# A fixed order of TensorE's phases in a mixture-of-experts kernel, with an expert's return in two halves inside the next expert

## The chip, the cores and the metric

The kernel runs on one core of a Trainium2 chip. The metric is the device time of one execution in microseconds, taken as the median of the runs shown. TensorE does the matmuls, VectorE (DVE), ScalarE (ACT) and GpSimd (POOL) the element-wise work, and SyncE (SP) issues the transfers of the weights.

## The reference, cut to what matters

A layer of a streaming encoder over 256 tokens of width 2048, all in float32: a mixer (attention beside a state-space scan), then 16 experts with two chosen per token, beside a gated per-layer embedding (PLE), and a normalisation behind each half. The change touches what comes after the mixer:

```python
def routed_experts(x, w_router, router_bias, w_gate, w_up, w_down):
    ...
    for e in range(N_EXPERTS):
        hid = jax.nn.silu(xt @ w_gate[e]) * (xt @ w_up[e])
        out = out + combine[:, e:e + 1] * (hid @ w_down[e])

def per_layer_embedding(x, p_i, w_ple, w_ple_gate):
    gate = jax.nn.sigmoid(jnp.einsum('bsd,de->bse', x, w_ple_gate))
    return gate * jnp.einsum('bsk,kd->bsd', p_i, w_ple)

        h = layer_norm(DEEPNORM_ALPHA * h + mix, ln1_g[i], ln1_b[i])
        moe = routed_experts(h, ...)
        ple = per_layer_embedding(h, p[i], w_ple[i], w_ple_gate[i])
        h = layer_norm(DEEPNORM_ALPHA * h + moe + ple, ln2_g[i], ln2_b[i])
```

## The kernel before

**Stages.** The mixer runs to about 429 us, the first normalisation and the router to about 458, the sixteen experts to about 1454, and the second normalisation and the output end the span at 1475.1.

**One expert.** An expert works on up to 64 of the 256 tokens. `gather` (L678 to L703) picks the rows of two experts at once by 32 matmuls of `h` with a one-hot tile `oh` (L692), so it runs ahead of experts 0, 2, 4 and so on; ScalarE and VectorE copy the result into `xg`. `gate_up` (L714 to L725) multiplies `xg` with eight weight tiles of 2 MiB, alternately of w_gate and w_up (L722, 64 matmuls, 128 instructions in the trace). `places` (L705 to L712) transposes the one-hots (L709) into `cm`. `hidden` (L727 to L737) forms silu(gate) x up (L729 to L731), transposes it by four matmuls (L734), and copies it to `hidT` (L736). `down` (L765 to L787) multiplies it with four tiles of w_down (L774, 32 matmuls), splits the product in a high and a low part `y` (L762, L763), and calls `give_back` (L739 to L753): sixteen matmuls of `cm` with `y` (L746) bring the rows back to their tokens, and eight VectorE instructions (L751) drain them, weighted, into `acc`.

**Beside the experts.** `ple_gate` computes a quarter c of the PLE at experts 3, 6, 9 and 12 (`PLE_AT`): 32 sums of hT with three tiles of w_ple_gate (L818, four, eight and four blocks) and eight products with p (L833). The first part of quarter 0 stands behind the router's matmuls (L623), by an `issue_after`. `residual` adds the scaled first normalisation: eight broadcasts of the gain and bias rows per quarter (L898), two VectorE passes (L909, L910), one POOL pass, at experts 4, 5, 7 and 8. At expert 13 the rows of the second norm are made in the same way. At expert 7 `overflow` holds a branch (L848) for experts with over 64 tokens, which isn't taken here.

**The weights.** All weight tiles of this half go through a ring of eight 2 MiB buffers, and one more that is used once. SP issues the loads in the fixed order of `plan_loads`: for each expert g0, u0, ... g3, u3, d0 to d3, and at a PLE expert its three PLE tiles ahead of g0. A load takes the buffer that `take`, in the order of the program, gave back the longest ago, and waits until TensorE has done the last matmul that reads it:

```python
    def fill(self, n=100):
        while self.spare and n and self.n < len(self.loads):
            j = self.spare.pop(0)
            key, load = self.loads[self.n]
            ...
    def take(self, key):
        t, j = self.tiles.pop(key)
        if j != self.once:
            self.spare.append(j)
        return t
```

**What sets the order.** The program text calls the steps expert by expert. Before, the tile scheduler arranges the instructions of each engine by its own estimates; so the PLE sums, the returns of an expert and the next expert's gate stand mixed on TensorE.

## Time and profile before

| | |
|---|---|
| median of 3 runs | 1473.13 us (1471.68 to 1480.07) |
| profiled execution, its own time | 1476.78 us |
| its span | 1475.1 us |
| TensorE busy, 6531 instructions | 1399.1 us, 95% |
| VectorE busy | 465.7 us, 32% |
| ScalarE busy | 297.9 us, 20% |
| weights' queue (q1) | 495.41 MB, 83.8% of 16 engines' span |
| granted clock of TensorE, mean | 0.98 |

The page gives busy time per engine over the whole span. The mixer and the experts have different limits, so the rows further down are of the stretch behind 440 us. [...] Times in rows are microseconds from the span's start.

### The profile page before, as it was taken

The page shows a single profiled execution, that of the slowest core. Times are in us where ns is not written, and L with a number is a line of the kernel's source. Part 1 is how long each engine was busy: PE and PEld are TensorE (multiplying, and loading weights), DVE is VectorE, ACT ScalarE, POOL GpSimd, SP SyncE. Part 2 cuts the span into 40 slices and gives each one's busy share as a digit, 9 for nine tenths or more (in the row PEclk, how much of TensorE's full clock was granted, in tenths as well). Part 3 has the DMA queues.
Part 4 walks back from the last instruction along what each step waited for, and adds up shares of the span by engine and source line. Part 5 has one row for each costly group of instructions (what it writes and reads, how often), then busy time and mean ns, then how long its engine had stood idle before and what let it go on. Part 6 is the DMA issues. An engine that isn't in the chain of part 4 may idle for free. (4 is left out here: it accounts for less than half of the span.)

```text
span 1475.1 us, 15513 instructions
## 1 busy us (share of the span) xinstructions
PE 1399.1 (95%) x6531; PEld 733.8 (50%) x6531; DVE 465.7 (32%) x777; ACT 297.9 (20%) x477; POOL 72.8 (5%) x90
## 2 busy tenths in 40 slices
PE   7999999999989999999999999899999999999994
PEld 5878888787784343334335333433333343353332
DVE  4386774546552211202123002222020220202117
ACT  4475554444340010001001000100010010011001
POOL 3000111201000000000000000000000000000002
PEclk9999999999999999999999999999999999999997
DMA  8645445456939999999999889999999999999993
GB/s 273 195 166 178 160 160 180 157 196 224 344 147 398 426 426 427 416 425 403 425 426 415 322 370 427 375 422 419 399 379 426 427 413 392 420 427 426 426 389 130
DMA packets 89711, 499.93 MB, mean 339 GB/s; under 512 B 9716, under 2 KB 22460, under 8 KB 65316
## 3 DMA queue, kind: packets, MB, share of 16 engines
q1 hardware_dynamic: 88128, 495.41, 83.8%
q0 software_dynamic: 1472, 3.43, 0.8%
q8 instruction: 53, 0.87, 0.2%
q14 instruction: 22, 0.18, 0.0%
q10 hardware_dynamic: 36, 0.05, 0.0%
HBM read 496.70 MB, written 2.16 MB: 338 GB/s over the span
## 5 line engine op out<-in xcount | busy, mean ns | idle before, releaser
L722 PE MATMUL pgu<-ring,xg 128*64 128x512 f32 x2048 | 473.2, 601 | 0.0
L722 PEld LDWEIGHTS pgu<-ring,xg 128*64 128x64 f32 x2048 | 144.4, 138 | 293.3 <-issue 292.5
L774 PE MATMUL py<-ring,hidT 128*64 128x512 f32 x960 | 209.3, 594 | 4.1 <-ACT hidT L736 4.1
L211 DVE TENSOR_TENSOR wl<-ring,wh 128x1024 fp32r<-128x1024 f32 x128 | 156.0, 1223 | 140.2 <-ACT wh L210 135.0
L210 ACT ACTIVATE wh<-ring 128x1024 fp32r<-128x1024 f32 x128 | 135.3, 1059 | 172.5 <-PE pj L217 145.8
L215 PE MATMUL pj<-wh,xh 128*128 128x512 f32 x384 | 154.1, 403 | 0.8 <-ACT xh L192 0.7
L216 PE MATMUL pj<-wl,xh 128*128 128x512 f32 x384 | 153.7, 401 | 0.0
L217 PE MATMUL pj<-wh,xl 128*128 128x512 f32 x384 | 153.1, 400 | 0.0
L730 DVE TENSOR_TENSOR hid<-hid,pgu 128x512 f32<-128x512 f32 x16 | 11.0, 687 | 434.1 <-ACT hid L729 434.1
L774 PEld LDWEIGHTS py<-ring,hidT 128*64 128x64 f32 x960 | 67.6, 137 | 134.8 <-issue 128.5
L818 PE MATMUL pl<-ring,hT 128*128 128x512 f32 x256 | 120.9, 608 | 0.0
L763 DVE TENSOR_TENSOR y<-py,y 128x512 fp32r<-128x512 f32 (+1 forms) x34 | 22.3, 657 | 238.8 <-ACT y L762 238.8
L729 ACT ACTIVATE hid<-pgu 128x512 f32<-128x512 f32 x16 | 9.6, 597 | 401.5 <-PE pgu L722 401.5
L215 PEld LDWEIGHTS pj<-wh,xh 128*128 128x128 f32 x384 | 72.7, 189 | 17.9 <-ACT xh L192 1.8
L217 PEld LDWEIGHTS pj<-wh,xl 128*128 128x128 f32 x384 | 72.6, 189 | 16.7 <-DVE xl L193 0.2
L216 PEld LDWEIGHTS pj<-wl,xh 128*128 128x128 f32 x384 | 72.8, 190 | 16.1
L818 PEld LDWEIGHTS pl<-ring,hT 128*128 128x128 f32 x256 | 45.1, 189 | 64.3 <-issue 64.1
L692 PE MATMUL mt<-oh,h 128*128 128x128 f32 x512 | 63.1, 287 | 5.0 <-PEq L848 5.0
L762 ACT ACTIVATE y<-py 128x512 fp32r<-128x512 f32 (+1 forms) x34 | 19.4, 572 | 229.7 <-PE py L774 200.1
L692 PEld LDWEIGHTS mt<-oh,h 128*128 128x128 f32 x512 | 62.3, 202 | 5.9 <-issue 5.7
L216 PE MATMUL pj<-wl,moh 128*128 128x512 f32 (+1 forms) x160 | 56.6, 354 | 0.5 <-DVE wl L211 0.5
L215 PE MATMUL pj<-wh,moh 128*128 128x512 f32 (+1 forms) x160 | 56.4, 355 | 0.6 <-ACT wh L210 0.6
(260 smaller groups left out, 1005.4 us busy)
## 6 DMA issues: line engine op xcount, KB each, us to landing
ring<-in_w_gate SPq DMA_DIRECT2D x64, 2048.0 KB, 18.2
ring<-in_w_up SPq DMA_DIRECT2D x64, 2048.0 KB, 17.8
ring<-in_w_down SPq DMA_DIRECT2D x60, 2048.0 KB, 16.5
ring<-in_w_in SPq DMA_DIRECT2D x48, 1024.0 KB, 5.1
ring<-in_w_out SPq DMA_DIRECT2D x16, 1024.0 KB, 5.8
ring<-in_w_ple_gate SPq DMA_DIRECT2D x16, 1024.0 KB, 20.6
ring<-in_w_down SPq DMA_DIRECT2D x32, 256.0 KB, 6.0
xq<-in_x SPq DMA_DIRECT2D x8, 256.0 KB, 9.6
```

The costliest lines, as they stand in the source:

```text
L210: nc.scalar.activation(h, v, AF.Copy)
L211: nc.vector.tensor_tensor(l, v, h.bitcast(F32), op=OP.subtract)
L215: nc.tensor.matmul(ps, ah, bh, start=first, stop=False)
L216: nc.tensor.matmul(ps, ah, bl, start=False, stop=False)
L217: nc.tensor.matmul(ps, al, bh, start=False, stop=last)
L692: nc.tensor.matmul(ps[:, k % 4], h[:, t, cols], oh[:, t, :, 0, :], start=t == 0, stop=t == 1)
L722: mm = nc.tensor.matmul(pgu[j][hs], xg[:, k, e % 2, :], w[:, r, fh * 512:(fh + 1) * 512], start=k == 0, stop=k == KB - 1)
L730: nc.vector.tensor_tensor(hid, hid, pgu[0], op=OP.mult)
L762: nc.scalar.activation(yh, ps, AF.Copy)
L763: nc.vector.tensor_tensor(yl, ps, yh.bitcast(F32), op=OP.subtract)
L774: nc.tensor.matmul(py[hs, c, :], hidT[:, j, fh * 64:(fh + 1) * 64], w[:, r, dh * 1024 + c * 512:dh * 1024 + (c + 1) * 512], start=fb == 0, ...
L818: nc.tensor.matmul(pg[t], hT[:, k, t * 128:(t + 1) * 128], w[:, k - k0, :], start=k == 0, stop=k == KB - 1)
```

## The change

**A fixed order.** A context manager `phase()` makes the instructions issued within it stand behind the last TensorE instruction of the phase before. Around `gate_up`, the return's two halves, the hidden transposes, the residual, the gather, the down and the PLE there is one each.

**Returns.** `down` ends with the split of y. An expert's return is made in the next expert's `hidden`: its half c = 0 between gate and hidden transposes, its half c = 1 behind them. The banks of the halves are ("mt", "pl") and ("gu", "mt").

**One-hots.** They are made one expert ahead (`onehot`) in the router's weight tile, no longer for two experts at once, and four small matmuls (L744) transpose them behind the first half of the return.

**PLE.** The quarter is computed in one piece behind the down. The first part of quarter 0 no longer stands behind the router, and its load comes ahead of expert 3, with the two others.

**Residual.** Four transposes of the normalised `hT` per token half take the place of the rows' broadcasts; one VectorE pass adds them to `acc`. It is at experts 2, 4, 5 and 7.

**Rows.** The four rows of gains and biases are no longer loaded in the mixer; those of the second norm are loaded by POOL's queue at expert 13. `hid`, `sg` and others have one buffer in place of two, `cm` has two, and `acc` is opened at expert 1.

```diff
-RES_AT = (4, 5, 7, 8)
+RES_AT = (2, 4, 5, 7)
+LN2_AT = 13
...
-    L.append((("pg", 0, 0), gate_part(0, 0)))
     for e in range(NE):
         if e in PLE_AT:
             c = PLE_AT.index(e)
-            L += [(("pg", c, g), gate_part(g, c)) for g in range(0 if c else 1, 3)]
+            L += [(("pg", c, g), gate_part(g, c)) for g in range(3)]
...
+    place = [None]
+
+    @contextmanager
+    def phase():
+
+        after = tc.issue_after(place[0]) if place[0] else ExitStack()
+        with after:
+            yield
+        place[0] = [i for i in nc.cur_bb.bb.instructions if i.engine == mybir.EngineType.PE][-1]
...
-    def hidden(pgu):
-        hid = mp.tile([128, 512], F32, name="hid", tag="w2", bufs=2)
+    def hidden(e, pgu, oh, between):
+
+
+        hid = mp.tile([128, 512], F32, name="hid", tag="w2", bufs=1)
...
-        ps = mt_psum([128, 4, 128])
+        with phase():
+            between(0)
+        hid_parts = phase()
+        hid_parts.__enter__()
+        ps2 = psum.tile([128, 2, 512], F32, name="py", tag="y", bufs=1)
+        ps, pc = ps2[:, 0, :].rearrange("p (j t) -> p j t", t=128), ps2[:, 1, :256]
+        for t in range(NT):
+            for _, hs in H2:
+                nc.tensor.matmul(pc[hs, t * 128:(t + 1) * 128], oh[:, t, e % 2, :], ident, start=True, stop=True)
...
-        return hidT
+        cm = mp.tile([128, 256], F32R, name="cm", tag="cm", bufs=2)
+        nc.scalar.activation(cm, pc, AF.Copy)
+        hid_parts.__exit__(None, None, None)
+        with phase():
+            between(1)
+        return hidT, cm
...
-        for c in range(2):
-            def pss(t):
-                if t == 0:
-                    return [mt_psum([128, 512]) for _ in range(2)]
-                p2 = psum.tile([128, 2, 512], F32, name="py", tag="y", bufs=1)
-                return p2[:, 0, :], p2[:, 1, :]
-            give_back(e, cm, y, c * 512, 512, pss)
+        return y
+
+    def return_half(e, cm, y, c):
+        def pss(t):
+            tag = (("mt", "pl"), ("gu", "mt"))[c][t]
+            return [psum.tile([128, 512], F32, name="bk", tag=tag, bufs=2) for _ in range(2)]
+        give_back(e, cm, y, c * 512, 512, pss)
...
-    with tc.issue_after(router_mm.ins):
-        ple_sums(0, range(1))
-    xg, oh = gather(0)
...
     def residual(c):
 
-        gain, bias = (row_bank(pl_psum(), lna[:, j, :], c).rearrange("p (f r) -> p r f", r=R) for j in range(2))
-        for t in range(NT):
-            part = mp.tile([128, 512], F32, name="part", tag="w2", bufs=2)
...
+        for t in range(NT):
+            ps = pl_psum()
+            for r in range(R):
+                nc.tensor.transpose(ps[:, r * 128:(r + 1) * 128], hT[:, R * c + r, t * 128:(t + 1) * 128], ident)
+            a = acc[:, t, c * 512:(c + 1) * 512].rearrange("p (f r) -> p r f", r=R)
+            nc.vector.scalar_tensor_tensor(a, ps.rearrange("p (r f) -> p r f", r=R), ALPHA, a, op0=OP.mult, op1=OP.add)
+
+    last = None
     for e in range(NE):
-        pgu, gated = gate_up(e, xg)
-        cm = places(e, oh)
-        hidT = hidden(pgu)
-        if e == 0:
+        if e % 2 and e + 1 < NE:
+            oh_next = onehot(e + 1)
+        with phase():
+            pgu = gate_up(e, xg)
+        if e == 1:
...
+        hidT, cm = hidden(e, pgu, oh, lambda c: last and return_half(*last, c))
         if e in RES_AT:
-            with tc.issue_after(gated.ins):
+            with phase():
                 residual(RES_AT.index(e))
         if e == OV_AT:
             overflow()
+            place[0] = None
+        if e == LN2_AT:
+            lnr = pT[:16].rearrange("p t (j f) -> p t j f", f=128)[:, 0]
+            for j, n in enumerate(("ln2_g", "ln2_b")):
+                nc.gpsimd.dma_start(lnr[:, j, :], i[n][0].rearrange("(k f) -> k f", f=128))
         if e + 1 < NE:
             if e % 2:
-                xg, oh = gather(e + 1)
-            down(e, hidT, cm)
+                with phase():
+                    oh = oh_next
+                    xg = gather(oh)
+            with phase():
+                last = e, cm, down(e, hidT)
...
         if e in PLE_AT:
-            ple_gate(PLE_AT.index(e))
+            with phase():
+                ple_gate(PLE_AT.index(e))
```

On TensorE, at expert 12, before, behind the returns of expert 11 (L818 the PLE sums, L722 the gate's and up's matmuls with the ring's tiles, L734 the hidden transposes, L774 the down):

```order
L709 MATMUL mt<-ident,oh 128x128 x2
L818 MATMUL pl<-ring_6632,hT 128x512 x4
L818 MATMUL pl<-ring_6634,hT 128x512 x8
L722 MATMUL pgu<-ring_6656,xg 64x512 x8
L818 MATMUL pl<-ring_6634,hT 128x512 x3
L722 MATMUL pgu<-ring_6737,xg 64x512 x8
L818 MATMUL pl<-ring_6634,hT 128x512 x3
L722 MATMUL pgu<-ring_6747,xg 64x512 x8
L818 MATMUL pl<-ring_6634,hT 128x512 x2
L818 MATMUL pl<-ring_6653,hT 128x512
L722 MATMUL pgu<-ring_6757,xg 64x512 x8
```

The same place now, from the last of expert 12's gate tiles to the first of expert 13 (L724 the gate's matmuls, L763 a half of the return, L744 the one-hots, L746 the hidden transposes, L790 the down, L832 and L842 the PLE):

```order
L724 MATMUL pgu<-ring_6787,xg 64x512 x8
L763 MATMUL bk<-y_6744,cm 128x512 x8
L744 MATMUL py<-ident,wr 64x128 x4
L746 MATMUL py<-ident,hid 128x128 x4
L763 MATMUL bk<-y_6744,cm 128x512 x8
L790 MATMUL py<-ring_6789,hidT 64x512 x8
...
L832 MATMUL pl<-ring_6579,hT 128x512 x8
L832 MATMUL pl<-ring_6581,hT 128x512 x16
L832 MATMUL pl<-ring_6600,hT 128x512 x8
L842 MATMUL mt<-ring_6600,pT 128x512 x4
L724 MATMUL pgu<-ring_6829,xg 64x512 x8
```

The PLE tiles are the three whose numbers stand ahead of the gate's in the order of the loads; they were read between the gate's tiles, and are read behind the four of the down.

On TensorE, behind the down of expert 13, before (L746 the returns, L722 the gate of expert 14):

```order
L774 MATMUL py<-ring_7076,hidT 64x512 x8
L746 MATMUL mt<-y_7229,cm 128x512 x4
L746 MATMUL mt<-y_7230,cm 128x512
L722 MATMUL pgu<-ring_7094,xg 64x512
L746 MATMUL py<-y_7229,cm 128x512 x4
L746 MATMUL mt<-y_7230,cm 128x512
L746 MATMUL mt<-y_7231,cm 128x512 x2
L722 MATMUL pgu<-ring_7094,xg 64x512 x4
L746 MATMUL py<-y_7230,cm 128x512 x2
L746 MATMUL py<-y_7231,cm 128x512 x2
L722 MATMUL pgu<-ring_7094,xg 64x512 x3
L709 MATMUL mt<-ident,oh 128x128 x2
```

And now, behind the gate of expert 14:

```order
L724 MATMUL pgu<-ring_7205,xg 64x512 x8
L763 MATMUL bk<-y_7207,cm 128x512 x8
L744 MATMUL py<-ident,wr 64x128 x4
L746 MATMUL py<-ident,hid 128x128 x4
L763 MATMUL bk<-y_7207,cm 128x512 x8
L790 MATMUL py<-ring_7278,hidT 64x512 x8
```

The return has left the place behind its own expert's down, and stands around the next expert's hidden transposes.

## Rows read from the trace of the kernel before

**Rows 1.** TensorE's waits from 440 us on: line, releaser, total us, times, longest.

```profile
PE mt L734 <- DVE hid L731: 9.1, 12, 0.8
PE mt L746 <- DVE acc L751: 8.5, 9, 1.0
PE mt L692 <- PEq L848: 5.0, 1, 5.0
```

**Rows 2.** Windows: length, busy us of five engines, granted clock, DMA share, GB/s.

```profile
442.00:1447.00 1005.00, 968.04 (x4386) 385.32 (x4388) 186.36 (x320) 77.33 (x162) 20.73 (x17) 0.98 0.98 408
995.34:1007.39 12.05, 12.05 (x50) 3.79 (x46) 2.42 (x4) 1.19 (x2) 0.00 (x0) 1.00 1.06 402
1125.61:1176.18 50.57, 47.24 (x214) 15.89 (x214) 9.08 (x17) 2.77 (x5) 0.00 (x0) 1.00 1.01 428
```

**Rows 3.** The page: GB/s in 40 equal slices of the span.

```profile
GB/s 273 195 166 178 160 160 180 157 196 224 344 147 398 426 426 427 416 425 403 425 426 415 322 370 427 375 422 419 399 379 426 427 413 392 420 427 426 426 389 130
```

**Rows 4.** Timeline of PE (start, us): hidden transposes, experts 3 and 12.

```profile
663.54 0.74 PE L734 MATMUL mt<-ident,hid 128*128 128x128 f32 x4 [0.79 <-DVE hid L731]
...
1260.26 0.74 PE L734 MATMUL mt<-ident,hid 128*128 128x128 f32 x4 [0.79 <-DVE hid L731]
```

**Rows 5.** Timeline of PE, experts 12 to 15: start, us, instructions.

```profile
1203.30 0.66 PE L746 MATMUL mt<-y,cm 64*128 64x512 f32 x4
...
1205.91 10.47 PE L818 MATMUL pl<-ring,hT 128*128 128x512 f32 x24
1216.30 3.65 PE L722 MATMUL pgu<-ring,xg 128*64 128x512 f32 x16
...
1323.36 7.39 PE L692 MATMUL mt<-oh,h 128*128 128x128 f32 x64
...
1382.77 13.95 PE L774 MATMUL py<-ring,hidT 128*64 128x512 f32 x64 [0.69 <-ACT hidT L736]
...
1434.87 0.44 PE L798 MATMUL py<-ring,hidT 128*64 128x256 f32 x2 [0.69 <-ACT hidT L736]
```

**Rows 6.** Timeline of SP: two loads issued during the gate of expert 14.

```profile
1370.29 0.33 SPq L82 DMA_DIRECT2D ring<-in_w_gate  x1
1373.72 0.33 SPq L82 DMA_DIRECT2D ring<-in_w_up  x1
```

**Rows 7.** DMA issues, 826 to 832 us: size, us from issue to landing.

```profile
ring<-in_w_up SPq DMA_DIRECT2D x1, 2048.0 KB, 7.8
```

**Rows 8.** Groups by line: busy us, mean ns of one, idle before.

```profile
L751 DVE SCALAR_TENSOR_TENSOR acc<-mt,cw,acc 128x512 f32<-128x512 f32 x56 | 40.1, 744 | 6.2 <-PE mt L746 5.9
L898 PE MATMUL pl<-lnr,ident 16*128 16x128 f32 x128 | 17.3, 280 | 0.0
```

**Rows 9.** Timeline of PE at the router.

```profile
442.55 5.40 PE L818 MATMUL pl<-ring,hT 128*128 128x512 f32 x12
448.05 0.37 PE L663 MATMUL mt<-s,tri 128*128 128x16 f32 x2
...
448.71 1.96 PE L818 MATMUL pl<-ring,hT 128*128 128x512 f32 x4
...
457.82 2.37 PE L722 MATMUL pgu<-ring,xg 128*64 128x512 f32 x10
```

**Rows 10.** More windows: TensorE's granted clock is third from last.

```profile
1399.80:1403.20 3.40, 3.40 (x9) 1.37 (x9) 0.90 (x3) 0.00 (x0) 0.00 (x0) 0.51 1.00 422
1396.40:1399.80 3.40, 1.54 (x7) 0.55 (x5) 1.81 (x3) 1.19 (x2) 0.00 (x0) 1.00 1.02 434
1125.60:1129.00 3.40, 1.96 (x10) 1.04 (x12) 0.69 (x1) 0.60 (x1) 0.00 (x0) 1.00 1.04 436
10.00:20.00 10.00, 8.53 (x27) 6.58 (x28) 6.26 (x8) 5.51 (x8) 6.78 (x15) 1.00 1.08 344
```

**Rows 11.** Timeline of SP at the overflow branch of expert 7.

```profile
923.12 0.33 SPq L82 DMA_DIRECT2D ring<-in_w_up  x1
951.97 0.34 SPq L82 DMA_DIRECT2D ring<-in_w_gate  x1
```

More of the change, by code (lines that the diff above doesn't have):

```diff
@@ L1 @@
-from contextlib import ExitStack
+from contextlib import ExitStack, contextmanager
 import concourse.bass as bass
@@ L161, in front @@
     nc.gpsimd.dma_start(cw[80:88], i["ssd_norm_w"][0].rearrange("(b f) -> b f", f=128))
-    lnr = const.tile([16, 4, 128], F32, name="lnr")
-    for j, n in enumerate(("ln1_g", "ln1_b", "ln2_g", "ln2_b")):
-        nc.gpsimd.dma_start(lnr[:, j, :], i[n][0].rearrange("(k f) -> k f", f=128))
-    fr.lnr = lnr
     lnT = const.tile([128, 2, KB], F32, name="lnT")
@@ L622, in back @@
     for t in range(NT):
-        router_mm = nc.tensor.matmul(pr[:, t, :], r4[:, t * 128:(t + 1) * 128], sel4, start=True, stop=True)
+        nc.tensor.matmul(pr[:, t, :], r4[:, t * 128:(t + 1) * 128], sel4, start=True, stop=True)
     rb = fr.rb
@@ L673, in back, with onehot, gather @@
     dbg("pos", pos)
+    place = [None]
[5 more added lines that the diff above has]
+        place[0] = [i for i in nc.cur_bb.bb.instructions if i.engine == mybir.EngineType.PE][-1]
     H2 = ((0, slice(0, 64)), (1, slice(64, 128)))
-    def gather(e):
-        oh = mp.tile([128, NT, 2, 2, CAP], F32, name="oh", tag="oh")
+    def onehot(e):
+        b = e // 2 % 2
+        oh = fr.wr.rearrange("p (b t j k) e -> p b t j (k e)", b=2, t=2, j=2)[:, b]
         for t in range(NT):
             for j in range(2):
-                nc.vector.tensor_scalar(oh[:, t, j], i1[:, None, :].to_broadcast([128, 2, CAP]),
-                                        pos[:, t, e + j:e + j + 1], None, op0=OP.is_equal)
+                nc.vector.tensor_scalar(oh[:, t, j], i1, pos[:, t, e + j:e + j + 1], None, op0=OP.is_equal)
+        return oh
+    def gather(oh):
         xg = mp.tile([128, KB, 2, CAP], F32, name="xg", tag="xg")
@@ L691, in gather @@
                 for t in range(NT):
-                    nc.tensor.matmul(ps[:, k % 4], h[:, t, cols], oh[:, t, :, 0, :], start=t == 0, stop=t == 1)
+                    nc.tensor.matmul(ps[:, k % 4], h[:, t, cols], oh[:, t], start=t == 0, stop=t == 1)
             if k4 % 2:
@@ L702, in gather @@
                 nc.vector.tensor_tensor(v, v, bias, op=OP.add)
-        return xg, oh
-    def places(e, oh):
-        ps = mt_psum([128, 256])
-        for t in range(NT):
-            nc.tensor.transpose(ps[:, t * 128:(t + 1) * 128], oh[:, t, e % 2].rearrange("p a b -> p (a b)"), ident)
-        cm = mp.tile([128, 256], F32R, name="cm", tag="cm")
-        nc.scalar.activation(cm, ps, AF.Copy)
-        return cm
+        return xg
     def gate_up(e, xg):
@@ L755, in y_parts @@
     def y_parts():
-        y0 = mp.tile([128, 2, 512], F32R, name="y0", tag="y")
-        y1 = [mp.tile([128, 512], F32R, name="y1", tag="w2", bufs=2) for _ in range(2)]
-        return (y0[:, 0, :], y0[:, 1, :]), y1
+        y = mp.tile([128, 2, 2, 512], F32R, name="y0", tag="y")
+        return [(y[:, c, 0, :], y[:, c, 1, :]) for c in range(2)]
     def split_y(y, ps, col, n):
@@ L763, in split_y, with down @@
         nc.vector.tensor_tensor(yl, ps, yh.bitcast(F32), op=OP.subtract)
-    def down(e, hidT, cm):
+    def down(e, hidT):
         py = psum.tile([128, 2, 512], F32, name="py", tag="y", bufs=1)
@@ L807, in down_last, with ple_gate @@
                     nc.vector.bn_stats(st[:, t, c, :], acc[:, t, c * 256:(c + 1) * 256])
-    pgs = {}
-    def ple_sums(c, parts):
-        pg = pgs[c] = pgs.get(c) or [pl_psum() for _ in range(NT)]
-        for g in parts:
-            k0, k1 = PLE_PARTS[g]
+    def ple_gate(c):
+        cs = slice(c * 512, (c + 1) * 512)
+        pg = [pl_psum() for _ in range(NT)]
+        for g, (k0, k1) in enumerate(PLE_PARTS):
             w = v2(ring.take(("pg", c, g)), 512)
@@ L821, in ple_sums @@
                 ring.fill()
-        return w[:, k1 - k0:k1 - k0 + 2, :] if k1 == KB else None
-    def ple_gate(c):
-        cs = slice(c * 512, (c + 1) * 512)
-        w = ple_sums(c, range(0 if c else 1, 3))
-        pg = pgs.pop(c)
+        w = w[:, k1 - k0:k1 - k0 + 2, :]
         for t in range(NT):
-            sg = mp.tile([128, 512], F32, name="sg", tag="w2", bufs=2)
+            sg = mp.tile([128, 512], F32, name="sg", tag="w2", bufs=1)
             nc.scalar.activation(sg, pg[t], AF.Sigmoid)
-            ps = pl_psum()
+            ps = mt_psum([128, 512])
             for k in range(2):
@@ L884, in overflow @@
                                                        acc[:, t, cs], op0=OP.mult, op1=OP.add)
-    with tc.issue_after(router_mm.ins):
-        ple_sums(0, range(1))
-    xg, oh = gather(0)
-    lna = fr.lnr[:, 0:2, :]
-    with tc.issue_after(stats_done.ins):
-        nc.vector.tensor_scalar(lna, lna, ALPHA, None, op0=OP.mult)
+    oh = onehot(0)
+    xg = gather(oh)
     def row_bank(ps, rows, c):
```

25 lines of the change are left out of this document (11 added, 14 removed).

## The prediction

> **What bounds the kernel now.** I read the waits first, then the transfers, then the order of time around the four per-layer-embedding (PLE) experts. The waits of TensorE from 440 us on are short and all on its own neighbours: 9.1 us for the hidden product, 8.5 us for the drains of a return, 5.0 us for the overflow branch, others less than 7 [rows 1]. None is on a transfer, so it looks as if TensorE alone set the pace. The windows say that this is only just so. From 442 to 1447 us TensorE is busy 968 of 1005 us, and the transfers run at 408 GB/s in the mean, where the undisturbed expert 11 shows 428 [rows 2] and most slices of the page 425 to 427 [rows 3]. By 427 GB/s the stream has 1005 x (1 - 408/427) = 45 us of idle time in all. A 2 MiB tile (2.097 MB) takes 4.91 us, an expert's twelve take 58.9 us, but TensorE goes through expert 11 in 50.57 us [rows 2]. So in every ordinary expert the stream falls 8 us behind, and it catches up where TensorE works on something else: the PLE sums and the gathers. The eight buffers carry the difference. From the hidden transposes of expert 3 to those of expert 12 the kernel takes 596.7 us, 198.9 for each period of three experts with one PLE part [rows 4]. The stream needs for such a period (the part is 4.72 MB, some 12.05 us by a window in which 402 GB/s moved as much [rows 2]) 3 x 58.9 + 12.05 = 188.8 us. A faster TensorE can therefore gain at most 10 us per period, and only if the stream never stops.
>
> **The change, part by part.** *PLE.* Before, the PLE matmuls stand among the gate's: 1205.91 shows 24 of them, 1216.30 sixteen of the gate, and so on to the hidden transposes at 1260.26 [rows 4, 5]. Each PLE tile is used up, and its buffer given back, while the gate runs. Now the three PLE tiles are still loaded ahead of the gate's first tile, but are taken only after that expert's down. For the gate and the down they occupy three of eight buffers. Two costs follow. First, ahead of the gate's last tile the stream has to bring 12.05 us of PLE data of which TensorE uses nothing yet. Second, after the gate, TensorE works for a long time on tiles that are there (down and PLE), while only the four buffers of the down, and then the PLE's own, come free: the stream stops.
>
> The prices. A PLE matmul takes (1216.30 - 1205.91)/24 = 0.433 us, 72 of them (64 sums, 8 of p) 31.2 us [rows 5]. A gate tile takes 3.43 us, the distance of two issues that each wait for one tile's last matmul [rows 6]; a gate 8 x 3.43 = 27.45. The down takes 13.75, its row less the overlap with the next, the gather 7.2 [rows 5]. A load issued into an idle stream lands 7.8 us later [rows 7].
>
> *Returns.* Before, the sixteen return matmuls begin right after the down, wait for y and for the drains, and the gate's matmuls fill in between; behind the down of expert 14, which ends near 1396.6 [rows 5], TensorE is busy 1.54 of 3.40 us [rows 10]. The change puts eight of them into the wait for the hidden product, and eight into the wait for its copy. Between gate and down there is then 1.33 + 0.45 + 0.74 + 1.33 = 3.9 us: eight returns at twice the row of four (0.66), the one-hots (four with half the columns, 0.37 to 0.74, taken as 0.45) and the four transposes (0.74) [rows 4], eight returns. An ordinary expert takes 27.45 + 3.9 + 13.75 = 45.1 us instead of 50.6. Where a gather follows, its banks come free only behind eight drains of 0.744 us on VectorE [rows 8], 6.0 us against 3.9: I put the lull at 6.5, and with the gather's 7.2 at 13.7. The bounds of that: 3.9 (the drains keep up) to 8 (they start only behind the hidden product).
>
> *Residual, row vectors, one-hots.* Eight transposes, twice 0.74 = 1.5 us, take the place of eight broadcast matmuls (17.3/64 = 0.27 each, 2.2 us [rows 8]), and one VectorE pass that of two and a POOL pass; TensorE's side is what counts, and it gains 0.7 four times, worth nothing where the stream is late anyway. The rows of the second norm come at expert 13 by POOL's queue, 32 such matmuls behind its lull, of which I leave eight to waits that are there anyway: 24 x 0.27 = 6.5 us. The one-hots move one expert earlier on VectorE, at nothing, since it is busy 186 of 1005 us [rows 2].
>
> *Router.* Sixteen PLE matmuls filled the wait for the router: 442.55 and 448.71 [rows 9]. [...] The first gate starts at about 459.3 instead of 457.82 [rows 9].
>
> *The sum*, on the profiled execution's span of 1475.1 us. The first buffer comes free at 459.3 + 3.43 = 462.7; the stream moves from 2.9 us later (7.8 - 4.91). To the gate of expert 3 there are 35 more tiles and the PLE part: 465.6 + 35 x 4.91 + 12.05 = 649.5, and with the last tile's 3.43 the gate ends at 652.9. TensorE alone would be there 20 us earlier, at 459.3 + 43.8 + 54.9 + 46.6 + 27.45 = 632 (expert 0 without returns in its lull, 1 with a gather, 2 with a residual, gate 3). Then 13.7 + 13.75 + 31.2 = 58.7 brings it to 711.6. The last PLE buffer is free only then; its load lands 7.8 later, and 24 tiles and a PLE part follow: 711.6 + 7.8 + 117.8 + 12.05 + 3.43 = 852.7 for the end of gate 6. A period is 199.8 us, against 198.9. Expert 6: 3.9 + 13.75 + 31.2, and 2 for a down tile that isn't there yet, 903.5; gate 7 to 931.0. There the overflow branch stops the stream: SP issues nothing from 923.12 to 951.97 [rows 11], and TensorE loses 5.0 us [rows 1]. With lull, residual and gather (6.5 + 1.5 + 5.0 + 7.2) the down starts at 951.2, its first buffer is free at 954.6, and 16 tiles and a PLE part give 954.6 + 7.8 + 73.7 + 12.05 + 3.43 = 1051.6 for gate 9. One more period: 1251.4 for gate 12. From there TensorE leads: 50.9 to 1302.3 with the PLE, expert 13 takes 27.45 + 13.7 + 13.75 + 6.5 = 61.4 to 1363.7, expert 14 to 1408.8, gate 15 and its lull to 1440.2. There the last down starts, which is at 1434.87 now [rows 5], and 40.2 us follow as before: 1480.4. In the stretches where TensorE leads there are eight lulls; a fall of the clock as in 1399.80:1403.20 costs 3.40 x 0.5 = 1.7 us [rows 10], and I take five, since 1396.40:1399.80 ahead of it was as empty as a lull will be, while the lull behind gate 10 was followed by none [rows 2, 10]: 8.5 us. That is 1488.9, 13.8 over 1475.1. The median of the runs shown is 1473.1 (the profiled execution took 1476.78 with what lies around its span), so 1487.
>
> In other words: TensorE's own stalls shrink by some 55 us, and in gates 3, 6, 9 and 12 it waits about 20, 10, 14 and 13 us for weights, where it never waited.
>
> The stream's rate carries most of this; it is 425 to 428 GB/s where nothing stops it [rows 2, 3]. [...]
>
> **The rivals.** *A: the stream never stops, faster.* If the buffers that the quicker experts give back early keep the stream at 427 GB/s through down and PLE, its 45 us of idle time [rows 2] are what is to be won. All of it gives 1430, a third 1460. It decides at the end of gate 3 and behind it: with waits at experts 3, 6, 9 and 12 under 37 us in sum (58 - 21) the kernel gets over 0.5% faster. Against it: of 58.7 us after gate 3 the stream can fill only what d0 to d3 and the first two PLE tiles give back, six tiles, 30 us.
> *B: no difference.* The waits are as I say but smaller, because the lulls with a gather are 3.9 instead of 6.5 us and no fall of the clock follows: 1487 - 8.5 - 4 x 2.6 = 1468 to 1478.
> *C: slower still, by the clock.* Each of the fifteen lulls is returns, transposes and waits, and the next stretch may run at half the clock as 1399.80:1403.20 did: eight instead of five where TensorE leads, and in the four gates that the stream paces, where TensorE pauses 1.5 us in each 4.91, a tile would take 6.9 us instead of 4.91 until the clock rises. 1487 + 3 x 1.7 + 4 x 2 to 4 gives 1500 to 1508. Against it: in 10:20 TensorE was busy 8.53 of 10 us at a granted clock of 1.00, and 1.96 of 3.40 us behind gate 10, with expert 11 at 1.00 throughout [rows 2, 10].
> [...]
> *D: the order isn't what it says.* The listing of instructions shows the PLE in one piece behind the down and the returns in two halves, so this gets no chance of its own.
>
> **How the numbers follow.** Forecast 62%, with 1475 to 1500; a fifth of that under the 0.5% line. A 10%, B 14%, C 14%. What a measurement tells from no change here is about 0.5%: 1465.8 to 1480.5. Faster: A, 0.10. Same: B and 0.12 of the forecast, 0.26. Slower: 0.64. The range leaves out A and the upper end of C: 1466 to 1503.
>
> **What would show it.** In the changed profile: waits of TensorE on a transfer, in gates 3, 6, 9 and 12 alone, 10 to 20 us each; tiles landing each 4.9 us with TensorE behind them in those gates; the stream idle for 15 to 20 us behind each of them; experts 10 and 14 at 45 us; gates ending near 653, 853, 1052 and 1251. Wrong it is if those waits are absent or under 37 us in sum, if ordinary experts take 48 us or more, or if the clock stays at 1.00 behind all lulls.

## The result

The changed kernel takes 1492.73 us (median of five runs, 1489.97 to 1495.47), the kernel before 1473.13 (five runs). The ratio is 1.0118, with a 95% interval of 1.0089 to 1.0148: slower by 1.2%, as forecast (1487, range 1466 to 1503). The profiled execution took 1492.86 us with a span of 1490.7, so the trace is that of a run like the others.

### The profile page after: what moved, and what is told of

Read it like the earlier page. It is cut to its first block, busy times and chain, and to the rows that moved or that the text cites. A ratio compares the mean times of both kernels' runs of the same rounds, so it can differ in the third digit from the quotient of the medians.

```text
span 1490.7 us, 15640 instructions
## 1 busy us (share of the span) xinstructions
PE 1369.6 (92%) x6595; PEld 741.5 (50%) x6595; DVE 454.1 (30%) x768; ACT 296.7 (20%) x477; POOL 62.1 (4%) x80
## 5 line engine op out<-in xcount | busy, mean ns | idle before, releaser
L724 PE MATMUL pgu<-ring,xg 128*64 128x512 f32 x2048 | 458.5, 604 | 54.7 <-DMA ring<-in_w_gate 38.9
L724 PEld LDWEIGHTS pgu<-ring,xg 128*64 128x64 f32 x2048 | 148.1, 139 | 361.4 <-issue 315.1
L790 PE MATMUL py<-ring,hidT 128*64 128x512 f32 x960 | 210.2, 594 | 4.5 <-DMA ring<-in_w_down 3.5
L734 DVE TENSOR_TENSOR hid<-hid,pgu 128x512 f32<-128x512 f32 x16 | 11.0, 687 | 433.2 <-ACT hid L733 433.2
L790 PEld LDWEIGHTS py<-ring,hidT 128*64 128x64 f32 x960 | 67.2, 137 | 137.4 <-issue 126.1
L832 PE MATMUL pl<-ring,hT 128*128 128x512 f32 x256 | 110.9, 594 | 0.0
L703 PE MATMUL mt<-wr,h 128*128 128x128 f32 x512 | 67.5, 299 | 16.1 <-DVE acc L768 7.1
L768 DVE SCALAR_TENSOR_TENSOR acc<-bk,cw,acc 128x512 f32<-128x512 f32 (+1 forms) x128 | 81.7, 711 | 1.9 <-PE bk L763 1.9
L832 PEld LDWEIGHTS pl<-ring,hT 128*128 128x128 f32 x256 | 48.3, 190 | 62.6 <-issue 62.6
L703 PEld LDWEIGHTS mt<-wr,h 128*128 128x128 f32 x512 | 66.0, 212 | 18.6 <-DVE acc L768 8.9
## 6 DMA issues: line engine op xcount, KB each, us to landing
ring<-in_w_gate SPq DMA_DIRECT2D x64, 2048.0 KB, 18.9
```

Source lines behind the costliest of these rows:

```text
L703: nc.tensor.matmul(ps[:, k % 4], h[:, t, cols], oh[:, t], start=t == 0, stop=t == 1)
L724: nc.tensor.matmul(pgu[j][hs], xg[:, k, e % 2, :], w[:, r, fh * 512:(fh + 1) * 512], start=k == 0, stop=k == KB - 1)
L768: nc.vector.scalar_tensor_tensor(a, ps[dh], cw[:, t, e:e + 1], a, op0=OP.mult, op1=OP.add)
L790: nc.tensor.matmul(py[hs, c, :], hidT[:, j, fh * 64:(fh + 1) * 64], w[:, r, dh * 1024 + c * 512:dh * 1024 + (c + 1) * 512], start=fb == 0, ...
L832: nc.tensor.matmul(pg[t], hT[:, k, t * 128:(t + 1) * 128], w[:, k - k0, :], start=k == 0, stop=k == KB - 1)
```

## The profile after

The page of the changed kernel, parts 1, 2 (GB/s in 40 slices) and 4 (the chain that ended last):

```profile
PE 1369.6 (92%) x6595; PEld 741.5 (50%) x6595; DVE 454.1 (30%) x768; ACT 296.7 (20%) x477; POOL 62.1 (4%) x80
...
GB/s 265 198 171 169 173 153 186 165 211 253 308 187 319 427 425 426 415 427 361 365 426 414 427 426 383 345 415 424 413 297 422 426 415 427 425 382 385 416 394 149
...
PE 27%; DMA 6%; DVE 2%; SPq 0%; ACT 0%; issue 0%; POOL 0%; DVEq 0%
```

TensorE is busy for 30 us less than before and the span is 16 us longer: it stands still more. From the thirteenth slice on, without the last, five of the stream's slices stand at 365 GB/s or less, before only one [rows 3], and the chain runs through transfers (DMA 6%), which it didn't before:

```profile
PE 34%; DVE 2%; ACT 0%; issue 0%; POOL 0%; DVEq 0%
```

TensorE's waits from 440 us on (line, releaser: total us, times, longest):

```profile
PE pgu L724 <- DMA ring<-in_w_gate: 38.9, 14, 13.2
PE pgu L724 <- DMA ring<-in_w_up: 15.8, 13, 1.3
PE mt L703 <- DVE acc L768: 7.1, 5, 1.9
PE mt L703 <- PEq L857: 6.1, 1, 6.1
PE mt L659 <- DVE s L653: 5.3, 1, 5.3
PE py L790 <- DMA ring<-in_w_down: 3.5, 4, 1.3
```

The waits of [rows 1] for the hidden product and for the drains of a return are gone (the 7.1 us left are the gather's banks). In their place stand 38.9 + 15.8 + 3.5 = 58.2 us for weights. Window by window they lie in gates 3 (19.9), 6 (10.6), 9 (11.8) and 12 (12.4) and in the downs of experts 6 and 12 (3.5).

Gate 3 and what follows it, TensorE's timeline (start, length, instructions, the idle time before):

```profile
617.40 9.33 PE L724 MATMUL pgu<-ring,xg 128*64 128x512 f32 x32 [13.23 <-DMA ring<-in_w_gate]
...
646.73 3.65 PE L724 MATMUL pgu<-ring,xg 128*64 128x512 f32 x16 [1.25 <-DMA ring<-in_w_gate]
651.64 3.65 PE L724 MATMUL pgu<-ring,xg 128*64 128x512 f32 x16 [1.25 <-DMA ring<-in_w_up]
655.23 1.19 PE L763 MATMUL bk<-y,cm 64*128 64x512 f32 x8
...
660.74 7.49 PE L703 MATMUL mt<-wr,h 128*128 128x128 f32 x64 [1.94 <-DVE acc L768]
668.16 13.95 PE L790 MATMUL py<-ring,hidT 128*64 128x512 f32 x64
682.04 27.73 PE L832 MATMUL pl<-ring,hT 128*128 128x512 f32 x64
...
713.14 2.37 PE L724 MATMUL pgu<-ring,xg 128*64 128x512 f32 x10
```

First TensorE waits 13.23 us: the PLE's three tiles are brought ahead of the tile it needs, while it needs none of them. Then the gate goes at the pace of the stream, one tile each 4.91 us. Then come 58 us of work on tiles that are there. What the stream did in those, SP's timeline and two windows (the last three figures are granted clock, DMA share, GB/s; after first, before second):

```profile
689.21 0.33 SPq L83 DMA_DIRECT2D ring<-in_w_up  x1
702.94 0.33 SPq L83 DMA_DIRECT2D ring<-in_w_gate  x1
713.24 0.33 SPq L83 DMA_DIRECT2D ring<-in_w_up  x1
```

```profile
652.00:713.00 61.00, 59.06 (x244) 28.57 (x240) 11.16 (x18) 5.68 (x13) 0.62 (x1) 1.00 0.87 362
```

```profile
652.00:713.00 61.00, 58.35 (x284) 24.46 (x280) 12.35 (x18) 6.87 (x15) 2.53 (x2) 0.97 0.98 410
```

689.21, 702.94 and 713.24 are the loads that wait for the first, second and third PLE tile to be read. Between them the stream has 4.91 us of work for 10 to 14 us of time. In four windows of 65 us from the end of gates 3, 6, 9 and 12 on:

```profile
655.00:720.00 65.00, 63.06 (x262) 30.06 (x262) 11.85 (x19) 6.27 (x14) 2.52 (x2) 1.00 0.86 352
855.70:920.70 65.00, 63.27 (x234) 25.13 (x234) 9.10 (x15) 3.26 (x6) 2.54 (x2) 1.00 0.96 401
1056.80:1121.80 65.00, 63.05 (x256) 31.20 (x256) 11.86 (x19) 6.27 (x14) 2.53 (x2) 0.97 0.83 340
1258.90:1323.90 65.00, 63.22 (x234) 25.10 (x234) 8.77 (x13) 3.26 (x6) 3.50 (x4) 1.00 0.95 401
```

Against 427 GB/s that is 11.4, 4.0, 13.2 and 4.0 us in which the stream stands still.

## The experiments

The experiments were run in three groups (E1 to E4, E5 to E8, E9 and E10), each beside the kernel before on the same chip. Its medians there were 1476.8, 1475.3 and 1475.4 us, and beside the changed kernel 1473.1. A difference of 2 or 3 us between rows of different groups is therefore not safe; the ratios are the better comparison.

| version | us | ratio to before | waits for weights, us |
|---|---|---|---|
| changed kernel | 1492.7 | 1.0118 (1.0089 to 1.0148) | 58.2 |
| E1, its PLE loads behind the down's | 1453.8 | 0.9844 (0.9822 to 0.9866) | 27.9 |
| E2, its PLE work ahead of the gate | 1453.1 | 0.9841 (0.9817 to 0.9864) | 26.9 |
| E3, its returns behind their own down | 1512.2 | 1.0231 (1.0207 to 1.0256) | 21.5 |
| E4, before, its PLE behind the down | 1494.5 | 1.0109 (1.0087 to 1.0132) | 16.8 |
| E5, PLE loads between gate and down | 1478.5 | 1.0022 (0.9993 to 1.0052) | 46.8 |
| E6, PLE loads one expert earlier | 1500.0 | 1.0155 (1.0092 to 1.0219) | 61.7 |
| E7, E2 with PLE work at the router | 1447.8 | 0.9818 (0.9762 to 0.9875) | 29.8 |
| E8, E2 with returns behind the down | 1483.4 | 1.0057 (1.0034 to 1.0081) | none |
| E9, changed kernel, residual of before | 1498.3 | 1.0146 (1.0114 to 1.0179) | 53.9 |
| E10, E2 with idle products at the router | 1450.2 | 0.9826 (0.9798 to 0.9854) | 22.8 |

### E1 and E2: the tiles are read in the order in which they are loaded

E1 moves the loads:

```diff
     for e in range(NE):
-        if e in PLE_AT:
-            c = PLE_AT.index(e)
-            L += [(("pg", c, g), gate_part(g, c)) for g in range(3)]
         for k in range(4):
...
             L += [(("d", e, q), quarter(i["w_down"][0, e], q)) for q in range(4)]
+        if e in PLE_AT:
+            c = PLE_AT.index(e)
+            L += [(("pg", c, g), gate_part(g, c)) for g in range(3)]
```

> The changed kernel with one edit: the three PLE tiles of an expert are loaded behind its down tiles instead of ahead of its gate tiles, so the loads stand in the order in which the tiles are read. The order of TensorE is that of the changed kernel. Theory (PLE tiles that are held while gate and down run stop the stream; TensorE then waits for weights at experts 3, 6, 9 and 12): the waits on transfers fall from 58.2 us to 5 to 25 us, the stream is idle some 40 us less, and the time is 1440 to 1460, below both kernels. Rival (the fixed order itself costs the time: lulls between gate and down, late drains ahead of the gather, falls of the clock; the waits for weights only fill what would be lost anyway): the waits fall, other waits grow, and the time stays at 1480 to 1495.

E2 moves the work instead:

```diff
     for e in range(NE):
...
+        if e in PLE_AT:
+            with phase():
+                ple_gate(PLE_AT.index(e))
         with phase():
             pgu = gate_up(e, xg)
...
-        if e in PLE_AT:
-            with phase():
-                ple_gate(PLE_AT.index(e))
```

> The changed kernel with one edit: the PLE quarter is computed in one piece ahead of its expert's gate instead of behind its down; the loads keep their order. So TensorE reads the tiles in the order in which they are loaded, by moving the work and not the loads. Theory (held PLE tiles): the same as with the loads moved, 1440 to 1460, waits on transfers 5 to 25 us, none of them in the gates of experts 3, 6, 9 and 12. Rival (the PLE in one piece is what hurts, since gate and PLE no longer alternate and the stream runs unevenly): waits of over 40 us at other gates, 1475 to 1495.

Measured: 1453.8 and 1453.1 us, 39 us under the changed kernel (40 by the ratios) and 1.6% under the kernel before. Two opposite moves with the same effect leave one cause, the distance between a PLE tile's load and its reading. The clock, in the changed kernel granted at 0.50 in 617.40:622.00 and at 1.00 in 622.00:640.00, is not a second one. Added up from windows of 1 us behind 440 us, as busy time x (1 - granted clock), it costs TensorE by estimate 20.0 us in the changed kernel, 11.5 in E1 and 12.7 in E2, and 7.9 of the changed kernel's lie at the start of gates 3, 6 and 9, where it waits for weights anyway. Windows of 442 to 1420 us, in the order before, after, E1:

```profile
442.00:1420.00 978.00, 943.48 (x4224) 373.75 (x4226) 179.13 (x302) 75.36 (x158) 20.73 (x17) 0.98 0.98 410
```

```profile
442.00:1420.00 978.00, 897.26 (x4198) 374.79 (x4200) 160.80 (x284) 72.80 (x156) 11.71 (x11) 0.97 0.96 402
```

```profile
442.00:1420.00 978.00, 926.83 (x4431) 389.02 (x4430) 172.77 (x307) 75.83 (x161) 11.73 (x11) 0.98 1.00 416
```

The rate goes from 402 to 416 GB/s (E2: 417). The waits for weights don't vanish: E2's longest is 1.3 us, and they are spread over 23 tiles.

```profile
PE pgu L724 <- DMA ring<-in_w_up: 13.1, 11, 1.3
PE pgu L724 <- DMA ring<-in_w_gate: 11.2, 10, 1.2
```

In gates 3, 6, 9 and 12, where E2 was to have none, it has none. They are now harmless in kind: the stream hardly stops, and TensorE follows it. I had expected 5 to 25 us; 27 is a little more, since TensorE is quicker than the stream as soon as nothing holds it (44.9 us for expert 11 of the changed kernel, against 58.9 for the transfer of twelve tiles at 4.91).

### E5 and E6: half the dose and double the dose

E5 puts the three loads between gate and down, E6 ahead of the gate of the expert before.

```diff
-        if e in PLE_AT:
-            c = PLE_AT.index(e)
-            L += [(("pg", c, g), gate_part(g, c)) for g in range(3)]
         for k in range(4):
...
+        if e in PLE_AT:                      # E5
+            c = PLE_AT.index(e)
+            L += [(("pg", c, g), gate_part(g, c)) for g in range(3)]
         if e < NE - 1:
```

> The changed kernel with the PLE tiles loaded between an expert's gate tiles and its down tiles, so that they are held over the down alone, not over gate and down. A middle dose. Theory (the time goes with how long unread PLE tiles hold buffers): between the changed kernel (1492.7) and the one with the loads behind the down (1453.8), some 16 us under the changed kernel: 1470 to 1482; waits on transfers 35 to 50 us. Rival (any load that stands ahead of its turn costs the same, the PLE's 12 us of stream ahead of tiles that are read earlier): 1485 to 1495.

> The changed kernel with the PLE tiles loaded one expert earlier, ahead of the gate of experts 2, 5, 8 and 11, so that they are held over two experts. A double dose. Theory in its simple form (cost grows with the time that the buffers are held): 1500 to 1530. Theory in the form of my sum (what costs is that the stream stands still while TensorE works from gate's end through down and PLE, and that is the same with five cycling buffers whether they cycle for one expert or two): 1490 to 1500, the waits for weights spread over experts 2 and 3, 5 and 6, and so on, 60 to 68 us in sum.

E5 gives 1478.5, between the two and below the rival's 1485 to 1495, with 46.8 us of waits, 30.1 of them now in the downs, because there the PLE's transfers stand ahead of what is needed next:

```profile
PE py L790 <- DMA ring<-in_w_down: 30.1, 11, 10.2
PE pgu L724 <- DMA ring<-in_w_up: 9.5, 8, 1.4
PE pgu L724 <- DMA ring<-in_w_gate: 7.2, 7, 1.3
```

E6 gives 1500.0 (1493.7 to 1502.4), on the line between the two forms of the theory, and the interval of its ratio overlaps that of the changed kernel. Its waits fit the form of the sum (61.7 us against 58.2, spread over two gates per PLE part), and holding the tiles twice as long didn't cost twice as much. In its profiled execution the router's first matmuls (L614) already start at 441.92 instead of 439.01, ahead of everything that the edit touches; over all the profiled executions this start lies between 438.3 and 441.9. So of the 9.3 us between the two spans at most 6.4 are of the load's place. The time alone doesn't decide it; the waits speak for a fixed price per PLE part.

### E4: the PLE's place alone, in the kernel before

```diff
-            down(e, hidT, cm)
+            downed = down(e, hidT, cm)
...
-            ple_gate(PLE_AT.index(e))
+            with tc.issue_after(downed.ins):
+                ple_gate(PLE_AT.index(e))
```

> The kernel before with one edit: an expert's PLE matmuls are queued on TensorE behind the last matmul of its down (the first part of quarter 0 too); loads, returns, residual and the scheduler's freedom elsewhere are those of before. Theory (holding the PLE tiles over gate and down is what costs): TensorE now waits for weights in the gates of experts 3, 6, 9 and 12, 20 to 35 us in sum, less than in the changed kernel since it is slower elsewhere, and the time is 1490 to 1503. Rival (the place of the PLE is worth nothing, and the changed kernel is slower by its lulls): 1470 to 1480, no waits for weights.

The edit is narrower than the expectation says: the first part of quarter 0 stays behind the router (the trace has its matmuls at 444.76 and 450.91), so at expert 3 only two of the three tiles are held.

1494.5: this one edit makes the kernel before as slow as the changed one. The waits for weights, which it had none of, are 16.8 us, less than I expected, and 12.5 of them stand in the gates of experts 3, 9 and 12:

```profile
PE pgu L722 <- DMA ring<-in_w_up: 7.3, 6, 1.3
...
PE pgu L722 <- DMA ring<-in_w_gate: 5.1, 5, 1.3
...
PE py L774 <- DMA ring<-in_w_down: 4.4, 4, 1.6
```

So not all of its 18 us need be waits. With no PLE matmuls among them, the returns of experts 2, 5, 8 and 11 stand bare behind the downs, and each time the clock falls into the next gate (614.50:621.30 is the first, at 0.50; the kernel before has 1.00 in this window). Added up as above, these four falls cost TensorE 12.3 us, in the very gates that may wait for weights; slow matmuls can take the place of waits there. Behind expert 13's down a stretch runs at a granted clock of 0.50, where TensorE has an instruction under way all the time:

```profile
1358.60:1375.70 17.10, 17.10 (x61) 10.90 (x63) 4.13 (x6) 2.98 (x5) 0.00 (x0) 0.50 0.62 261
```

By 0.50 of 17.10 us I estimate the loss there at 8.5 us. But the kernel before has falls of its own, one of them at the same place, behind expert 13's down (0.51):

```profile
1348.60:1352.00 3.40, 3.40 (x12) 1.49 (x13) 1.69 (x3) 0.00 (x0) 0.00 (x0) 0.51 1.03 439
```

Behind 440 us they cost it 17.2 us in all, added up as above, and E4 19.7 without its four falls into the gates. E4's span is 20.9 us longer than that of before: 2.2 stand ahead of the router, whose first matmuls start at 441.17 instead of 438.96, and some 2.5 are the clock outside these gates. The rest, some 16 us, comes with the PLE's new place. How it divides between the held buffers and the bare returns this run doesn't show.

### E3 and E8: what the returns in halves are worth

The same edit on the changed kernel (E3) and on E2 (E8): the sixteen return matmuls in one piece behind their own down.

```diff
-        hidT, cm = hidden(e, pgu, oh, lambda c: last and return_half(*last, c))
+        hidT, cm = hidden(e, pgu, oh, lambda c: None)
...
                 last = e, cm, down(e, hidT)
+            for c in range(2):
+                with phase():
+                    return_half(*last, c)
```

> The changed kernel with one edit: the sixteen return matmuls of an expert stand in one piece right behind its own down, no longer in two halves around the next expert's transposes. Theory (the halves save TensorE some 5 us per ordinary expert and 3 us where a gather follows, worth something only in the stretches where TensorE leads and not the stream): TensorE's own waits grow by some 60 us, the waits for weights shrink from 58 to some 30, the time is 1510 to 1525. Rival (the stream sets the time almost everywhere, so the return's place is worth nothing): 1488 to 1500.

> The version with the PLE ahead of the gate (1453.1) with the returns in one piece behind their own down. The same edit as on the changed kernel, where it cost 19.5 us. Theory (in the changed kernel the waits for weights swallowed a good part of what the halved returns save; with the stream running through, the return's place is worth more): TensorE sets the time again, no or few waits for weights, and the time is 1480 to 1496, that is 27 to 43 us over the version it is made from. Rival (the place of the return is worth the same 20 us wherever the PLE stands): 1470 to 1476.

Both times lie in the ranges of their theories. The edit costs 19.5 us on the changed kernel (17 by the ratios) and 30.3 us on E2 (32). E8's waits show what comes back, none of it for weights:

```profile
PE bk L763 <- ACT y L778: 12.7, 19, 0.8
PE pgu L724 <- DVE acc L768: 10.7, 9, 1.3
```

Without the waits for weights the time is 1490.7 us in E3 and 1434.5 in the changed kernel, 1483.4 in E8 and 1426.2 in E2. So the halves save TensorE 56 to 57 us of its own time on either version. In the changed kernel 36.7 of them come back as waits for weights (21.5 us in E3, 58.2 with the halves), in E2 26.9. E3's expectation had all of it as waits: TensorE's own waits, listed from 440 us on, grow by 28 us and not by 60; its busy time grows by 27.

### E7 and E10: the wait for the router

E7 takes E2 and puts the first part of the first PLE quarter back behind the router, where the kernel before has it; with it go the residual's experts (4, 5, 7 and 8, as before) and other banks for the first two returns. E10 puts eight idle products there, that free no buffer; their result is not used.

```diff
     L = ring.loads                                    # E7
     L.append(("p", rows(i["p"][0, 0], 0, 256, 0, 256)))
+    L.append((("pg", 0, 0), gate_part(0, 0)))
...
+    with tc.issue_after(router_mm.ins):
+        ple_sums(0, range(1))
     oh = onehot(0)
...
-            tag = (("mt", "pl"), ("gu", "mt"))[c][t]
+            tag = ("mt", "gu")[t] if e < 2 else (("mt", "pl"), ("gu", "mt"))[c][t]
```

```diff
+    with tc.issue_after(router_mm.ins):               # E10
+        fl = [pl_psum() for _ in range(NT)]
+        for k in range(4):
+            for t in range(NT):
+                nc.tensor.matmul(fl[t], hT[:, k, t * 128:(t + 1) * 128], h[:, t, k * 512:(k + 1) * 512],
+                                 start=k == 0, stop=k == 3)
     oh = onehot(0)
```

> The version with the PLE ahead of the gate (1453.1), with the first part of the first PLE quarter put back behind the router's matmuls, as in the kernel before, its load ahead of all others, the residual at experts 4, 5, 7 and 8 and other banks for the first two returns (since the PLE sums hold two banks). Theory (the router's gap costs TensorE 2 us at the lower clock, and the stream, which has all buffers full there, up to 8 us; this version is paced by the stream from the first gate on): the first gate starts at 457.5 to 458.5 instead of 459.7, the stream's gap ahead of it shrinks from 8 to some 2 us, and the time is 1444 to 1450. Rival (these gaps are made up later): 1451 to 1455.

> The version with the PLE ahead of the gate (1453.1) with eight idle products (hT with h, into two banks that nobody reads) behind the router's matmuls, where the kernel before has eight PLE sums. They keep TensorE at work in the router's wait but free no buffer, so they split the 5.3 us that the router's PLE part was worth. Theory (the clock is worth 2 us there, the buffer the rest): the gather takes 7.4 instead of 9.5 us, the first gate starts at 457.5 to 458.2, the stream's gap at the first release stays at 8 us, and the time is 1450 to 1452. Rival (all of it was the clock): 1447 to 1449; rival (all of it was the freed buffer): 1453.

The changed kernel at the router, TensorE's timeline, and the granted clock there (third from last in the window):

```profile
448.08 0.58 PE L659 MATMUL mt<-s,tri 128*128 128x16 f32 x2 [5.34 <-DVE s L653]
...
450.44 9.49 PE L703 MATMUL mt<-wr,h 128*128 128x128 f32 x64 [0.93 <-DVE wr L691]
459.86 3.65 PE L724 MATMUL pgu<-ring,xg 128*64 128x512 f32 x16
```

```profile
444.50:454.70 10.20, 5.69 (x26) 5.64 (x27) 5.76 (x33) 0.00 (x0) 0.00 (x0) 0.50 1.01 430
```

And there E2, E10 and E7:

```profile
450.65 9.15 PE L703 MATMUL mt<-wr,h 128*128 128x128 f32 x64 [0.93 <-DVE wr L691]
459.73 0.65 PE L724 MATMUL pgu<-ring,xg 128*64 128x512 f32 x2
```

```profile
449.87 7.38 PE L703 MATMUL mt<-wr,h 128*128 128x128 f32 x64
457.18 6.23 PE L724 MATMUL pgu<-ring,xg 128*64 128x512 f32 x28
```

```profile
450.16 7.39 PE L704 MATMUL mt<-wr,h 128*128 128x128 f32 x64
457.48 5.80 PE L725 MATMUL pgu<-ring,xg 128*64 128x512 f32 x26
```

E10 gives 1450.2, E7 1447.8, both in the ranges of their theories. E2 gave 1453.1, but the three come from different groups, and the intervals of the three ratios overlap. The traces divide the difference better. From the router's first matmuls (at 439.20, 438.32 and 438.62) to the first gate E2 takes 20.5 us, E10 and E7 18.9: 1.7 us, in the gather (9.15 against 7.38). I put them down to the clock, as an estimate from the changed kernel, where the gather took 9.49 us with 0.50 granted in 450.44:454.70, while the kernel before had 1.00 in 444.50:454.70 and a gather of 7.38. From the first gate to the end of the span E2 and E10 take 991.4 and 991.3 us, E7 988.5: 2.8 us for the freed buffer, together with the residual's other experts and the other banks, which no run separates from it. E7 has the lowest median, 1.8% under the kernel before: it keeps the changed kernel's fixed order, and reads the PLE's tiles in the order of their loads.

### E9: the residual

The residual of before (row broadcasts, two VectorE passes, one POOL pass) in the changed kernel:

```diff
+        gain, bias = (row_bank(pl_psum(), lna[:, j, :], c).rearrange("p (f r) -> p r f", r=R) for j in range(2))
         for t in range(NT):
-            ps = pl_psum()
-            for r in range(R):
-                nc.tensor.transpose(ps[:, r * 128:(r + 1) * 128], hT[:, R * c + r, t * 128:(t + 1) * 128], ident)
...
+            nc.vector.tensor_tensor(pv, h[:, t, c * 512:(c + 1) * 512].rearrange("p (r f) -> p r f", r=R), gain, op=OP.mult)
+            nc.vector.tensor_tensor(pv, pv, bias, op=OP.add)
...
+            nc.gpsimd.tensor_tensor(a, a, part, op=OP.add)
```

> The changed kernel with the residual computed as in the kernel before (rows broadcast by TensorE, two VectorE passes and one POOL pass per token half), at the changed kernel's experts. Theory (the residual is off what sets the time, except at expert 7, where TensorE leads): TensorE pays 0.7 us more four times, VectorE some 6 us more per residual, of which expert 5's and 7's may hold up the gather's banks by up to 3 us each; the time is 1491 to 1499, within 0.5% of the changed kernel. Rival (the new residual is a real part of what the change gains): over 1500.

1498.3 (five runs, 1494.2 to 1502.0) against 1492.7 (1490.0 to 1495.5), within the expected band and at its upper end; the intervals of the two ratios overlap. Most of what the trace shows is at expert 7, where the gather waits 4.17 us more behind the branch (the trace names no releaser). The residual from the transposed h is thus worth some 5 us or less, and is no part of the loss.

## Why the prediction was right

**The hold.** The step that carries the forecast is that PLE tiles loaded ahead of the gate and read behind the down make the stream stop. E1, E2 and E5 show it from three sides, and E4 supports it with its waits. The sum's ends of gates against the trace (the first return's start, or the last down's):

| | predicted | measured |
|---|---|---|
| gate 3 | 652.9 | 655.2 |
| gate 6 | 852.7 | 855.7 |
| gate 9 | 1051.6 | 1056.8 |
| gate 12 | 1251.4 | 1258.9 |
| last down | 1440.2 | 1450.6 |
| span, with 8.5 us for the clock | 1488.9 | 1490.7 |

Waits for weights in gates 3, 6, 9 and 12: 20, 10, 14 and 13 predicted, 19.9, 10.6, 11.8 and 12.4 measured. The ordinary expert 11 takes 44.9 us from gate's end to gate's end, forecast 45.1, before 50.57 [rows 2]. The forecast has the clock's 8.5 us in one term at the end, while the measured ends have the falls in them; that is part of why the differences grow from 2 to 10 us. The 5.8 us between 1487 and the measured 1492.7 are 1.8 of the span and 3.7 by which the profiled execution of the kernel before lay above its median; the rest lies around the span.

**The stop itself** was over-sized. The prediction's sign was a stream idle for 15 to 20 us behind each of the four gates; measured were 11.4, 4.0, 13.2 and 4.0 us. Its argument against rival A was that the stream can fill only six tiles, 30 us, in the 58.7 us behind gate 3. It left out the buffers that the gate itself had just given back: from 655.20 to 711.60 the stream moved 20.7 MB (367 GB/s for 56.4 us), nearly ten tiles. The sum of times doesn't use the six. It counts the 24 tiles behind the last PLE tile, and this count held. Its price of a PLE part is a little high as well: 12.05 us at 402 GB/s are 4.84 MB and not 4.72.

**TensorE's own time** came out right as a whole: 13.8 us over the span of before, less 57 of waits for weights, are 43 us saved, and 15.6 - 58.2 = 42.6 were measured. They are not mostly stalls, as the prediction has it. TensorE's own waits from 440 us on shrink from 38.2 to 24.7 us, and its busy time by 29.5.

**The router.** The sum starts with 459.3 for the first gate, a term that no run shows; in the changed kernel it was 459.86. The gather ahead of it took 9.49 instead of 7.38 us, at a granted clock of 0.50 up to about 454.7, that is for 4.3 us.

**The lulls.** 5.5 us from gate 3's end to the gather's start, where I had put 6.5 out of 3.9 to 8. One ordinary lull is 3.5 us.

**The rows of the second norm** were the one term that was clearly too small: 6.5 forecast, 1.60 + 2.54 + 5.49 = 9.6 us measured, with a stretch at half the clock in it, which is counted under the clock below, too:

```profile
1364.00 2.54 PE L901 MATMUL pl<-pT,ident 16*128 16x128 f32 x20
1366.47 1.07 PE L724 MATMUL pgu<-ring,xg 128*64 128x512 f32 x2
1367.48 5.49 PE L901 MATMUL pl<-pT,ident 16*128 16x128 f32 x32
```

```profile
1369.50:1376.30 6.80, 6.80 (x25) 4.17 (x25) 0.00 (x0) 1.79 (x3) 0.00 (x0) 0.50 0.86 366
```

**The clock** came out near the right sum by luck, by other places than I named. I had five falls of 1.7 us behind lulls where TensorE leads. Behind an ordinary lull there was none: the stretch with expert 10's lull and down is at 1.00 (1144.00:1161.20 below). Nor was there one behind the lulls with the residual's eight transposes at experts 4 and 5 (1.00 in 744.00:747.00 and 789.00:793.00). Behind a lull with late banks there is one at gates 9 and 11 (0.50 in 1062.30:1065.70 and 1195.40:1198.80; the gathers there take 9.11 instead of 7.49 us), and the second is swallowed by gate 12's wait for weights. A longer one follows the overflow branch (0.50 in 942.80:949.60), where the kernel before has one, too (0.50 in 931.00:935.00; its gather there took 9.76 us), and one lies in the norm's rows (0.50 in 1369.50:1376.30). Others came while TensorE waited for weights, at the start of gates 3, 6 and 9 (0.50 in 1019.00:1022.00 for gate 9):

```profile
1144.00:1161.20 17.20, 17.20 (x92) 6.87 (x94) 6.34 (x11) 0.87 (x2) 0.00 (x0) 1.00 1.01 428
...
816.50:823.30 6.80, 5.44 (x14) 1.91 (x16) 0.00 (x0) 0.00 (x0) 0.00 (x0) 0.50 1.01 424
...
608.30:622.00 13.70, 4.59 (x12) 1.64 (x14) 0.00 (x0) 0.00 (x0) 0.00 (x0) 0.50 1.03 427
```

Where TensorE leads, that is 1.6 us (gate 9, 9.11 - 7.49) + 2.4 (branch, 9.88 - 7.49; in 942.80:949.60 TensorE was busy 4.91 of 6.80 us) + 3.4 (norm's rows, half of 6.80) = 7.4 us. The last two rows cost next to nothing: TensorE was slow while it waited for tiles anyway, and once the gate ran at the stream's pace the clock was back (1.00 in 622.00:640.00, 823.30:850.00 and 1026.80:1050.00). So rival C fell: the clock did fall at the start of three of the four gates that the stream paces, but their ends are set by the last tile's landing (the waits of 1.25 us at 646.73 and 651.64 in gate 3); gate 12 started at 1.00 (1221.00:1224.40).

**Rival A**, that the stream never stops, was right about the size of the prize and wrong that the change as made gets it: 1430 to 1460 was its range, E1, E2 and E7 are at 1453.8, 1453.1 and 1447.8.

The stream moved at 427 to 428 GB/s where nothing stopped it, before (1125.61:1176.18 [rows 2]) and after (the row 608.30:622.00 above), and the prediction's tiles of 4.91 us stand (4.91 from 646.73 to 651.64 in gate 3).

## What to carry to other kernels

Where a ring of buffers feeds an engine that is nearly matched to its transfers, a tile should be read in the order in which it was loaded: one that is loaded early and read late takes a buffer from the stream twice, once as dead transfer time ahead of what is needed, and once as a stop behind it (here 58.2 us of waits for weights against 26.9, and 39 us of time). A saving on the compute engine is swallowed wherever the stream sets the pace (here 37 of some 56 us), so both rates belong in the estimate, stretch by stretch. Moving work out of the gaps of another loop also takes away what kept the buffers coming free (362 instead of 410 GB/s in 652.00:713.00 here), and can leave stretches behind that run at a lower clock (at the router, in 444.50:454.70, the granted clock was 1.00 with the PLE's sums and 0.50 without them).

## What the hardware showed that I had not expected

In this case TensorE had an instruction under way all the time and was still held at a lower clock. In 1358.60:1375.70 of E4 it was busy 17.10 of 17.10 us at a granted clock of 0.50, with broadcasts of 16 rows and returns of 64 rows for the first 11 us and matmuls of the gate behind them; in 1369.50:1376.30 of the changed kernel 6.80 of 6.80 us at 0.50, in and behind broadcasts of 16 rows. Whether the few rows are the cause no run tests: in 1144.00:1161.20 of the changed kernel returns of 64 rows run at 1.00. A busy share of 1 was thus no sign of the full clock, 1.00; the granted clock has to be read beside it.
